# A delta-rule scan beside other matrix work: matmul-free steps tied to TensorE's chunk steps, gate rows in a buffer of their own, output weights split unscaled, MLP differences one step earlier

## The chip, the core and the metric

The kernel runs on one NeuronCore of a Trainium2 chip. The core has five engines that run side by side, each taking its own instructions in order: TensorE (PE in the profile; its weight loads are shown as PEld), VectorE (DVE), ScalarE (ACT), GpSimd (POOL) and SyncE (SP), which here issues all DMA transfers. The metric is the device time of one execution in microseconds (us); the time before is the median of three runs.

## What is computed

One layer of a hybrid block for 128 context tokens and 2048 latent tokens of width 1024. The mixer puts four heads of a gated delta-rule scan (run forwards and backwards) beside four groups of a spatially gated MLP, and both share an input and an output projection; a squared-ReLU MLP of width 4096 follows.

```python
def gated_delta_chunked(q, k, v, g, beta, s0):
    ...
    g = jnp.cumsum(to_chunks(g), axis=-1)
    diff = g[..., :, None] - g[..., None, :]
    decay = jnp.where(incl, jnp.exp(jnp.where(incl, diff, 0.0)), 0.0)
    a_mat = jnp.where(strict, jnp.einsum('bnhcd,bnhsd->bnhcs', k_beta, k) * decay, 0.0)
    sol = lax.linalg.triangular_solve(a_mat + jnp.eye(DN_CHUNK, dtype=f32), rhs, ...)
    ...
    def step(S, xs):
        v_new = u_c - jnp.einsum('bhck,bhkv->bhcv', w_c, S)
        o = jnp.einsum('bhck,bhkv->bhcv', qd, S) + jnp.einsum('bhcs,bhsv->bhcv', qk_c, v_new)
        S = S * jnp.exp(gl)[..., None, None] + jnp.einsum('bhck,bhcv->bhkv', kd, v_new)
...
    o_a = rmsnorm(o_a, o_norm_l) * jax.nn.silu(gate.reshape(B, T, H_A, DV))
    u = jax.nn.gelu(u)
    vg = layernorm_noaffine(jax.nn.gelu(vg)...)
    mixed = jnp.einsum('gts,bnsgc->bntgc', ws_l, vg) + bs_l.T[None, None, :, :, None]
    o_b = u * mixed
    out = jnp.concatenate([o_a, o_b], axis=-1)
    return out @ w_out_l, s_new
...
    x = x + ga1 * o
    h = rmsnorm(x, norm_ffn_l) * (1.0 + sc2) + sh2
    x = x + ga2 * (jnp.square(jax.nn.relu(h @ w_ff1_l)) @ w_ff2_l)
```

## The kernel before

**Number format.** A float32 operand is split into a high part `h` and a rest `lo`; a product takes three matmuls (high by high, high by rest, rest by high; `mm3`, L221 to L223). ACT casts the high part and DVE subtracts it to get the rest, for weights in `split_w` (L195, L196) as for activations.

**Three stages.** The first (to about 445 us) normalises the rows and projects q, k and v, with the convolution. The second (about 445 to 1270 us) is the scan with all that is woven into it, and it is where the change lies. The third is the MLP, whose products go by a seven-product scheme on halves; its operands are sums and differences of the normalised rows, made and stored in `hop_d` by `h2_steps`.

**The scan.** There are 34 units: 17 token tiles of 128 rows forwards, then the same backwards. Unit number i has *prep* steps, which solve the triangular system of its chunk without the state, and four *scan* steps, which need the state of unit i - 1. The first prep step makes `E`, the decays, out of a row of cumulated g that is broadcast to all partitions (ACT, L1016 and L1017) and masks it twice on POOL (`Es` L1019, `E` L1021). The second multiplies the key products `KK` by it (DVE, L1029), sets the diagonal (POOL, L1031), casts the result to float16 as `AH` (ACT, L1034) and cuts the first blocks out as `X` (DVE, L1035). The third turns `X` into `Y` on PE (L1041, evicted by ACT at L1043). Then come five levels of two steps each, every one a few small PE matmuls with an eviction that the next step needs: L1061 with the predicated copy `P` on DVE (L1065), and L1072 and L1075 with the casts of `Y` and `X` on ACT (L1076, L1077). Four more steps end in `T` (L1119, L1122). Below, the PE work of prep and scan steps is called a chunk step, and these matmuls chunk matmuls.

**What is woven in.** Forwards, PE's large share is fill: the projections for gate, v and u of the gMLP (`f2_steps`; 576 steps, 62 of them ahead of the scan), whose weights are `W2`. Backwards it is the output projection (`o_steps`, weights `WO`) and for tiles 9 to 16 the making of the MLP's operands (`h2_steps`; `put`, L877 to L880, casts, subtracts and stores a pair `opH`, `opL`, in the four staging buffers that raw weights use too).

**Order.** The order is written by hand as events with a time, in units of one scan unit (`at`, `spread`). Unit i's prep steps lie between i - 2.46 and i - 0.03 (backwards i - 2.63 and i + 0.06), evenly. A scheduler then places the instructions on the engines by event order, but lets any instruction go earlier that is ready earlier. `emit` ties what may not: the first PE instruction of a fill step stays behind the chunk matmul that was emitted last (or three back, in the backward half). Steps of other kinds that issue no PE instruction (the first prep step, weight splits, `put`s) have no such tie. A tie makes no wait on the chip; it sets the order in which instructions stand in the engines' queues.

**Loads.** Rows of g (for `E`) and of exp g (for turning q, L1153) both come through `load_rows`, three buffers of one tag. The eight u weights are loaded and split at -8.5, ahead of the scan. The sixteen output weights are loaded, multiplied by a column of scales on DVE (L194) and split between 17.58 and 18.3, where the forward half ends. Each load waits for a staging buffer (four of them) and, in order, for whatever stands ahead of it in SP's queue.

Of the kernel before, what the change touches and what calls it, by code (L numbers as in the profile page):

```python
# [18 lines left out]
P = 128  # L19
# [38 lines left out]
AHEAD = 3  # L58
WINDOWS = [2.46, 0.03, -0.51, 1.06, -1.61, 18.16, 17.58, 18.3,
# [4 lines left out]
def hybrid_step(  # L64
# [55 lines left out]
    nhalf = cp.tile([P, 80], F32, name="nhalf")  # L120
# [42 lines left out]
    wscale = cp.tile([P, KT], F32, name="wscale")  # L163
# [25 lines left out]
    def split_w(raw, scale=None, pool=None, tag="w"):  # L189
# [3 lines left out]
        if scale is not None:  # L193
            V.tensor_scalar_mul(raw, raw, scale)  # L194
# [4 lines left out]
    def load_split(src, scale=None):  # L199
        return split_w(raw_w(src, sp, "raw"), scale)  # L200

    W2 = {"g": [], "v": [], "u": []}

    def load_w2(gi, k):
        off = {"g": 1536, "v": 2576, "u": 2064}[gi]
        W2[gi].append(load_split(w_in[0, k * P : (k + 1) * P, off : off + 512]))
# [75 lines left out]
    with ExitStack() as ph:  # L282
# [432 lines left out]
        def second_mods():  # L715

            load(out=wsT, in_=w_spatialT)
            V.tensor_copy(wscale[:, 0:4], vec[:, 68:69].to_broadcast([P, 4]))
            V.memset(wscale[:, 4:8], 0.5)
# [102 lines left out]
    def h2_steps(t, psum, tmp, wide=w512, part=None, half=None, src=None, own=None):  # L822
# [107 lines left out]
    with ExitStack() as ph:  # L930
# [26 lines left out]
        def load_rows(src, t, d):  # L957
            gb = q32("gb", 3)
# [22 lines left out]
        def unit(t, d, fresh=False, last=False):  # L981
# [11 lines left out]
            def prep_loads():  # L993
                u["gb"] = load_rows(g_d, t, d)
# [5 lines left out]
            def scan_loads():  # L1000
# [6 lines left out]
                u["eg"] = load_rows(eg_d, t, d)  # L1007
# [18 lines left out]
            def _():  # L1026
                a = u["KK"]
                for h in range(H):
# [3 lines left out]
                                base=0, channel_multiplier=-1)  # L1032
                u["AH"], u["AL"], u["X"] = f16("AH", BA), f16("AL", BA), f16("X", BX)
                A.copy(u["AH"], a)  # L1034
# [271 lines left out]
        def o_steps(du):  # L1306
# [22 lines left out]
            def trans(half):  # L1329
                def f():  # L1330
# [11 lines left out]
                    A.copy(hs, ps)  # L1342
                    V.tensor_tensor(out=ls, in0=ps, in1=f32(hs), op=ALU.subtract)
# [97 lines left out]
        for gi in "vu":  # L1441
# [555 lines left out]
```

## Time and profile before

| | |
|---|---|
| median of three runs | 2627.44 us (2621.16 to 2628.88) |
| the profiled execution's own time | 2625.06 us |
| its span in the trace | 2623.1 us |
| mean granted clock of PE in it | 0.994 |
| PE's share of the chain that ended last | 81% |

The trace is of one execution. In the tables of stretches, each engine's busy time stands in us, then the number of instructions in brackets; PEclk is the clock that PE was granted, 1.00 being full speed; then the share of the DMA engines' time and GB/s. In lists of instructions the columns are start, duration, engine, line and operation, output<-input, shape, count, and in square brackets how long that engine stood idle before it and what released it. In groups of instructions the total busy time in us and the mean in ns follow the count. In lists of waits stand the total, how often, and the longest.

### The profile page before, as it was taken

The page shows a single profiled execution, that of the slowest core. Times are in us where ns is not written, and L with a number is a line of the kernel's source. Part 1 is how long each engine was busy: PE and PEld are TensorE (multiplying, and loading weights), DVE is VectorE, ACT ScalarE, POOL GpSimd, SP SyncE. Part 2 cuts the span into 40 slices and gives each one's busy share as a digit, 9 for nine tenths or more (in the row PEclk, how much of TensorE's full clock was granted, in tenths as well). Part 3 has the DMA queues.
Part 4 walks back from the last instruction along what each step waited for, and adds up shares of the span by engine and source line. Part 5 has one row for each costly group of instructions (what it writes and reads, how often), then busy time and mean ns, then how long its engine had stood idle before and what let it go on. Part 6 is the DMA issues. An engine that isn't in the chain of part 4 may idle for free.

```text
span 2623.1 us, 44123 instructions
## 1 busy us (share of the span) xinstructions
PE 2566.0 (98%) x15330; PEld 2150.2 (82%) x15330; DVE 1777.2 (68%) x3605; ACT 1238.7 (47%) x3086; POOL 253.4 (10%) x478
## 2 busy tenths in 40 slices
PE   8999999899999999899999999999999999999998
PEld 4899999688888778778888788888887888888887
DVE  5867745666667778786578786677675544774874
ACT  4655555555556557664245543333342432342441
POOL 3112112111112122111000000000000000000000
PEclk9999999999999999999999999999999999999999
DMA  8867637645556658896777879445369978786782
GB/s 298 285 213 220 198 110 234 217 152 163 167 167 180 191 186 246 256 281 186 279 235 236 249 229 328 146 137 152 118 204 370 338 265 281 263 255 213 237 262 94
DMA packets 533861, 579.79 MB, mean 221 GB/s; under 512 B 35500, under 2 KB 366684, under 8 KB 530054
## 3 DMA queue, kind: packets, MB, share of 16 engines
q1 hardware_dynamic: 533638, 576.98, 68.9%
q8 instruction: 120, 1.97, 0.3%
q14 instruction: 103, 0.84, 0.1%
HBM read 397.62 MB, written 179.22 MB: 220 GB/s over the span
## 4 chain that ended last, share of the span: by engine, by line
PE 81%; DMA 8%; DVE 4%; ACT 3%; issue 2%; SPq 1%; POOL 0%; DVEq 0%; POOLq 0%; ACTq 0%
PE f L221 15%; PE f L222 15%; PE f L223 15%; PE pj L221 7%; PE pj L223 6%; PE pj L222 6%; PE pd L991 3%; PE pm L221 1%; PE pm L223 1%; PE pm L222 1%; DMA r<-in_w_ff_dram 1%; PE pt L590 1%; PE pd L1176 1%; PE pd L1175 1%; DMA raw<-in_w_mod_dram 1%
## 5 line engine op out<-in xcount | busy, mean ns | idle before, releaser
L221 PE MATMUL f<-hop,zH 128*128 128x512 f32 x960 | 373.7, 390 | 2.4 <-ACT zH L1500 2.4
L223 PE MATMUL f<-hop,zL 128*128 128x512 f32 x960 | 373.6, 389 | 0.0
L222 PE MATMUL f<-hop,zH 128*128 128x512 f32 x960 | 373.2, 389 | 0.0
L221 PE MATMUL f<-hop,wH 128*128 128x512 f32 x896 | 351.7, 393 | 2.4 <-ACT x L1576 2.4
L222 PE MATMUL f<-hop,wH 128*128 128x512 f32 x896 | 349.5, 391 | 0.0
L223 PE MATMUL f<-hop,wL 128*128 128x512 f32 x896 | 344.7, 390 | 0.0
L1500 ACT CAST zH<-zraw 128x512 fp32r<-128x512 f32 x240 | 146.9, 620 | 290.8 <-DVE zraw L1494 89.4
L221 PEld LDWEIGHTS f<-hop,zH 128*128 128x128 f32 x960 | 180.2, 188 | 41.2 <-ACT zH L1500 4.0
L223 PEld LDWEIGHTS f<-hop,zL 128*128 128x128 f32 x960 | 180.2, 188 | 39.0 <-DVE zL L1494 1.7
L222 PEld LDWEIGHTS f<-hop,zH 128*128 128x128 f32 x960 | 180.2, 188 | 37.2
L1494 DVE TENSOR_TENSOR zL<-zraw,zH 128x512 fp32r<-128x512 f32 x240 | 162.7, 688 | 68.7 <-ACT zH L1500 55.9
L221 PEld LDWEIGHTS f<-hop,wH 128*128 128x128 f32 x896 | 168.8, 188 | 36.6 <-ACT x L1576 2.8
L223 PEld LDWEIGHTS f<-hop,wL 128*128 128x128 f32 x896 | 168.5, 188 | 35.6
L222 PEld LDWEIGHTS f<-hop,wH 128*128 128x128 f32 x896 | 169.0, 189 | 32.5
L223 PE MATMUL pj<-kH,wL 128*128 128x386 f32 (+2 forms) x568 | 190.5, 335 | 0.0
L221 PE MATMUL pj<-kH,wH 128*128 128x386 f32 (+2 forms) x568 | 189.1, 335 | 0.3 <-DVE kH L488 0.3
L222 PE MATMUL pj<-kL,wH 128*128 128x386 f32 (+2 forms) x568 | 189.3, 333 | 0.0
L180 POOL TENSOR_TENSOR r<-rsq,nhalf 128x1 f32<-128x1 f32 (+1 forms) x38 | 22.8, 600 | 1379.1 <-DVE rsq L179 1379.1
L1647 ACT CAST wH<-s 128x512 fp32r<-128x512 f32 x96 | 58.9, 620 | 173.0 <-DVE s L1494 173.0
L538 DVE SCALAR_TENSOR_TENSOR cv<-pj,vec,cv 128x384 f32<-128x384 f32 (+2 forms) x164 | 87.2, 539 | 58.2 <-ACT cv L535 56.8
L1065 DVE CAST_PREDICATED P<-om,pd 128x256 f16<-128x256 uint16 x170 | 71.0, 428 | 64.4 <-PE pd L1061 63.5
L221 PEld LDWEIGHTS pj<-kH,wH 128*128 128x128 f32 x568 | 107.1, 189 | 4.6 <-issue 4.2
(409 smaller groups left out, 5889.8 us busy)
## 6 DMA issues: line engine op xcount, KB each, us to landing
zraw<-z_d SPq DMA_DIRECT2D x212, 256.0 KB, 4.6
raw<-in_w_ff_dram SPq DMA_DIRECT2D x128, 256.0 KB, 4.8
hop<-hop_d SPq DMA_DIRECT2D x28, 1024.0 KB, 11.4
z_d<-c SPq DMA_DIRECT2D x96, 256.0 KB, 2.4
zraw<-s_d SPq DMA_DIRECT2D x96, 256.0 KB, 5.0
raw<-in_w_mod_dram SPq DMA_DIRECT2D x80, 256.0 KB, 4.3
r<-in_w_ff_dram SPq DMA_DIRECT2D x80, 256.0 KB, 5.3
s_d<-s SPq DMA_DIRECT2D x64, 256.0 KB, 3.2
```

Of the source, the lines that this page charges most:

```text
L221: T.matmul(ps, lh, rh, start=first and i == 0, stop=False, skip_group_check=more)
L222: T.matmul(ps, lh, rl, start=False, stop=False, skip_group_check=more)
L223: T.matmul(ps, ll, rh, start=False, stop=last and i == n - 1, skip_group_check=more)
L538: V.scalar_tensor_tensor(out=cv[:, o : o + m], in0=ps[:, s + sh : s + sh + m], scalar=convw[:, w, j : j + 1], in1=cv[:, o : o + m], op0=AL ...
L590: T.matmul(ps[:, i * P : (i + 1) * P], kTt[:, i * P : (i + 1) * P], rhs[:, i * P : (i + 1) * P], start=True, stop=True)
L991: T.matmul(p[:, h, :], lhs[:, h, :], rhs[:, h, :], start=True, stop=True)
L1065: V.copy_predicated(out=half(u["P"], yi), mask=half(bc4(om[s]).bitcast(U16), yi), data=pp)
L1175: T.matmul(p[:, h, :], u["qT"][:, h, :], s[:, h, :], start=True, stop=False)
L1176: T.matmul(p[:, h, :], u["QK"][:, h, :], u["vn"][:, h, :], start=s is None, stop=True)
L1494: V.tensor_tensor(out=out, in0=a, in1=b, op=op)
L1500: A.copy(h, src)
L1647: A.copy(h, s2)
```

## The change

1. **Ties for steps without matmuls.** In `emit`, a step that issues no PE instruction and isn't fill now gets, for each of its DVE, ACT and POOL instructions, the same kind of tie: behind the first PE instruction of the chunk step emitted last.
2. **The second prep step is cut in two**, so that the cast to `AH` and the making of `X` form a step of their own; a unit then has 18 prep steps, not 17, in the same stretch.
3. **Rows of g** get a tag of their own (`gr`, one buffer, in the pool that holds the prep tiles); rows of exp g keep three (`eg`).
4. **Weights.** `wscale` and its multiplications go. Three raw weights are loaded at -8.5; then one weight is split at a time, u from -2 on and the output weights from 16.4 on, 0.12 units apart, and each split issues the next load. The scale moves into the eviction of the transposed rows in `o_steps`: ACT's cast becomes an activation with a scale, DVE's subtraction a scalar_tensor_tensor.
5. **MLP differences.** In `h2_steps` each subtraction stands one step earlier than the `put` that needs it.

```diff
+COMPUTE = (mybir.EngineType.DVE, mybir.EngineType.Activation, mybir.EngineType.Pool)
...
-    def split_w(raw, scale=None, pool=None, tag="w"):
+    def split_w(raw, pool=None, tag="w"):
...
-        if scale is not None:
-            V.tensor_scalar_mul(raw, raw, scale)
         A.copy(h, raw)
         V.tensor_tensor(out=lo, in0=raw, in1=f32(h), op=ALU.subtract)
...
         def plain():
             put(1, u[0])
             put(2, u[1])
+            u["d"] = part("d")
+            sub(u["y"][1], u["y"][0], u["d"])
 
         def third():
             put(3, u["y"][1])
-            d = part("d")
-            sub(u["y"][1], u["y"][0], d)
-            put(7, d)
+            put(7, u["d"])
+            sub(u["y"][0], u[0])
 
         def fifth():
-            sub(u["y"][0], u[0])
             put(5, u["y"][0])
+            sub(u["y"][1], u["y"][0])
 
         def sixth():
-            sub(u["y"][1], u["y"][0])
             put(6, u["y"][1])
+            sub(u[1], u["y"][1])
 
         def fourth():
-            sub(u[1], u["y"][1])
             put(4, u[1])
...
             def prep_loads():
-                u["gb"] = load_rows(g_d, t, d)
+                u["gb"] = load_rows(g_d, t, d, "gr", 1, pp)
...
-                u["eg"] = load_rows(eg_d, t, d)
+                u["eg"] = load_rows(eg_d, t, d, "eg", 3)
...
+
+            @prep.append
+            def _():
                 u["AH"], u["AL"], u["X"] = f16("AH", BA), f16("AL", BA), f16("X", BX)
-                A.copy(u["AH"], a)
+                A.copy(u["AH"], u["KK"])
                 V.tensor_tensor(out=u["X"], in0=u["AH"], in1=bc4(sg2), op=ALU.mult)
...
-        def load_wo(n, k):
-            if k == 0:
+        wlist = [("u", k) for k in range(KT)] + [(n, k) for n in range(2) for k in range(KT)]
+        wraw = []
+
+        def ahead():
+            if len(wraw) < len(wlist):
+                n, k = wlist[len(wraw)]
+                src = w2_src(n, k) if n == "u" else w_out[0, k * P : (k + 1) * P, n * 512 : (n + 1) * 512]
+                wraw.append(raw_w(src, sp, "raw"))
+
+        def split_next(j):
+            n, k = wlist[j]
+            if n != "u" and k == 0:
                 ga1.append(wrow(mod_d[1:2, 2 * D + n * 512 : 2 * D + n * 512 + 512]))
                 WO.append([])
-            WO[n].append(load_split(w_out[0, k * P : (k + 1) * P, n * 512 : (n + 1) * 512], wscale[:, k : k + 1]))
+            (W2 if n == "u" else WO)[n].append(split_w(wraw[j]))
+            ahead()
...
-                    A.copy(hs, ps)
-                    V.tensor_tensor(out=ls, in0=ps, in1=f32(hs), op=ALU.subtract)
+                    scale = 0.5 if half else vec[:, 68:69]
+                    A.activation(hs, ps, AF.Copy, scale=scale)
+                    V.scalar_tensor_tensor(out=ls, in0=ps, scalar=scale, in1=f32(hs), op0=ALU.mult, op1=ALU.subtract)
...
-        for gi in "vu":
-            for k in range(NV if gi == "v" else 0, KT):
-                at(-9 if gi == "v" else -8.5, lambda gi=gi, k=k: load_w2(gi, k))
+        for k in range(NV, KT):
+            at(-9, lambda k=k: load_w2("v", k))
+        for _ in range(3):
+            at(-8.5, ahead)
+        for j in range(len(wlist)):
+            at(-2 + 0.12 * j if j < KT else 16.4 + 0.12 * (j - KT), lambda j=j: split_next(j))
...
-        spread(p2[6], p2[7], [lambda n=n, k=k: load_wo(n, k) for n in range(2) for k in range(KT)], None)
...
             f()
+            made = tc.nc.cur_bb.bb.instructions[start:]
+            pe = [x for x in made if x.engine == mybir.EngineType.PE]
+            if hist and not pe and kind != "fill":
+                for x in made:
+                    if x.engine in COMPUTE:
+                        tc.add_manual_dep(x, hist[-1].name, mybir.DependencyInfo(
+                            mybir.DependencyClass.NoSync, mybir.DependencyReason.DATA), reason="order")
```

More of the change, by code (lines that the diff above doesn't have):

```diff
@@ L119, in hybrid_step @@
     V.tensor_copy(ident16, ident)
-    nhalf = cp.tile([P, 80], F32, name="nhalf")
+    nhalf = cp.tile([P, 88], F32, name="nhalf")
     V.memset(nhalf, -0.5)
@@ L197, in split_w, with load_split, w2_src @@
         return h, lo
-    def load_split(src, scale=None):
-        return split_w(raw_w(src, sp, "raw"), scale)
+    def load_split(src):
+        return split_w(raw_w(src, sp, "raw"))
     W2 = {"g": [], "v": [], "u": []}
+    def w2_src(gi, k):
+        off = {"g": 1536, "v": 2576, "u": 2064}[gi]
+        return w_in[0, k * P : (k + 1) * P, off : off + 512]
     def load_w2(gi, k):
-        off = {"g": 1536, "v": 2576, "u": 2064}[gi]
-        W2[gi].append(load_split(w_in[0, k * P : (k + 1) * P, off : off + 512]))
+        W2[gi].append(load_split(w2_src(gi, k)))
     def w512(name, dt=F32):
```

8 lines of the change are left out of this document (2 added, 6 removed).

## The prediction

> **What bounds the kernel now.** I read the page's first part, then busy time by stretches of the scan stage, then PE's gaps one by one in the timeline, and last the list of waits.
>
> ```profile
> span 2623.1 us, 44123 instructions
> PE 2566.0 (98%) x15330; PEld 2150.2 (82%) x15330; DVE 1777.2 (68%) x3605; ACT 1238.7 (47%) x3086; POOL 253.4 (10%) x478
> ```
>
> PE is busy for 2566.0 of 2623.1 us, and the change takes no matmul away. What it can win is PE's idle time, and what PE loses by a slower clock around it. The stretches (row: length, then busy time of PE, PEld, DVE, ACT, POOL, then PE's clock):
>
> ```profile
> 470.00:490.00 20.00, 12.59 (x75) 9.12 (x74) 10.18 (x21) 8.36 (x20) 1.54 (x2) 0.74 0.80 269
> 510.00:600.00 90.00, 87.61 (x752) 72.07 (x751) 57.12 (x160) 51.89 (x144) 14.18 (x18) 1.00 0.52 158
> 600.00:860.00 260.00, 260.00 (x2268) 216.25 (x2267) 173.08 (x482) 146.87 (x397) 46.07 (x58) 1.00 0.57 169
> 860.00:950.00 90.00, 78.70 (x665) 63.00 (x664) 65.29 (x167) 49.23 (x135) 14.08 (x17) 0.94 0.65 210
> 1020.00:1200.00 180.00, 167.71 (x1460) 137.03 (x1458) 142.18 (x333) 125.18 (x385) 35.29 (x42) 0.99 0.87 272
> ```
>
> Idle time of PE, length less busy: 7.4 us at the start of the scan (call it A), 2.4 in 510 to 600 (B), 11.3 around the turn from forwards to backwards (C), 12.3 where tiles 16 to 9 run backwards (D); together 33.4. Clock loss, busy time by (1 - clock): A 12.59 x 0.26 = 3.3, C 78.70 x 0.06 = 4.7, D 167.71 x 0.01 = 1.7; together 9.7. So the ceiling of the gain is **43 us**. The 260 us between 600 and 860 have no idle time to give.
>
> **A.** The first unit's chain:
>
> ```profile
> 471.26 0.40 PE L1041 MATMUL pd<-ident,X 128*128 128x128 f16 x4
> 474.35 0.62 ACT L195 CAST wH<-raw 128x512 fp32r<-128x512 f32 x1 [2.76 <-DMA raw<-in_w_in_dram]
> 476.38 0.58 ACT L1043 CAST Y<-pd 128x512 f16<-128x512 f32 x1
> 477.01 0.37 PE L1061 MATMUL pd<-Y,AH 128*128 128x64 f16 x4 [5.35 <-ACT Y L1043]
> ```
>
> PE finished the `X` product at 471.66; its eviction (0.58 us) began only at 476.38, because a cast of a u weight stood ahead of it in ACT's queue, waiting for its transfer. Such waits, in the whole scan stage:
>
> ```profile
> ACT E L1016 <- DMA gb<-g_d: 58.5, 26, 5.9
> DVE d L883 <- DMA y<-h_d: 16.1, 4, 5.5
> DVE raw L194 <- DMA raw<-in_w_out_dram: 9.3, 8, 2.3
> ```
>
> All three are, like A's cast, instructions that went early and then held an engine that chunk steps need. But most of the 58.5 us fell where PE had fill enough: the stretch 600 to 860 shows it. So a wait that goes is worth only the gap of PE that it ends in.
>
> **The change part by part.** *Weights at A*: u is no longer split ahead of the scan, but one weight at a time with three loads in flight. Of the gap of 5.35 us the eviction itself must stay (0.58 us and a hand-over, say 0.8), and of the other 2 us of A I leave 0.5 for the next steps' own evictions. Best gain: 7.4 - 1.3 + 3.3 = 9.4. The fourth load is only issued at the first split, and the splits start just where PE has no fill; if ACT meets it as it met the old one, 2.76 us come back. I take **7** (range 3 to 9).
>
> *B*: ties keep a unit's `E` (four ACT instructions and an exp) from standing ahead of another unit's casts. I take **1.5** of 2.4.
>
> *Weights at C*:
>
> ```profile
> 865.48 0.48 DVE L194 TENSOR_SCALAR raw<-raw,wscale 128x512 f32<-128x512 f32 x1 [2.31 <-DMA raw<-in_w_out_dram]
> 866.97 0.28 PE L1072 MATMUL pd<-P,X 128*128 128x64 f16 x4 [0.86 <-DVE P L1065]
> 891.60 0.28 PE L1061 MATMUL pd<-Y,AH 128*128 128x64 f16 x4 [3.04 <-ACT Y L1076]
> 932.91 0.28 PE L1061 MATMUL pd<-Y,AH 128*128 128x64 f16 x4 [0.54 <-ACT Y L1043]
> 939.11 0.37 PE L1061 MATMUL pd<-Y,AH 128*128 128x64 f16 x4 [0.66 <-ACT Y L1076]
> ```
>
> DVE stood in the multiplication by the scale waiting for a weight, and the copy that PE needed came late. That wait goes with the multiplication, and the splits start at 16.4 instead of 17.58. The largest gap, 3.04 us, is mixed: DVE was busy with gMLP fill, which gets no tie, and one weight subtraction. The timeline's gaps of C that end behind an output weight or a waiting `E` (five, from the 0.86 to the 0.54 above) come to 2.7 us; those where such work is one of several (six, from the 3.04 to the 0.66) come to 7.3, of which I count half, as of the 4.7 of clock. 2.7 + 3.6 + 2.3 gives **8.5** of 16.0 (range 3 to 13).
>
> *The operations themselves*:
>
> ```profile
> L194 DVE TENSOR_SCALAR raw<-raw,wscale 128x512 f32<-128x512 f32 x16 | 8.1, 508 | 9.4 <-DMA raw<-in_w_out_dram 9.3
> L1343 DVE TENSOR_TENSOR oL<-pm,oH 128x512 fp32r<-128x512 f32 x21 | 14.3, 688 | 11.8 <-ACT oH L1342 11.7
> L1242 DVE SCALAR_TENSOR_TENSOR gw<-gw,pj 128x512 f32<-128x512 f32 x10 | 6.8, 682 | 6.3 <-ACT gw L1241 6.3
> ```
>
> Sixteen multiplications go, 8.1 us of DVE, in no other sum than C's. The eviction with a scale costs what it did: a scalar_tensor_tensor out of PSUM took 682 ns, the subtraction 688. ACT's scaled copy of this size is not in the trace; the cast and ACT's other 128x512 operations lie near 0.6 us, and I take 0 (between -1 and +3 us over 34 evictions, off the path while DVE follows ACT with slack).
>
> *The `put`s and differences at D*:
>
> ```profile
> 1024.42 0.28 PE L1061 MATMUL pd<-Y,AH 128*128 128x64 f16 x4 [0.34 <-ACT Y L1076]
> ...
> 1102.98 0.69 DVE L883 TENSOR_TENSOR d<-y 128x512 f32<-128x512 f32 x1 [5.50 <-DMA y<-h_d]
> 1106.13 0.50 PE L221 MATMUL pm<-wH,oH 128*128 128x512 f32 x1 [1.14 <-DVE tmp L1362]
> 1121.72 0.62 ACT L877 CAST opH<-d 128x512 fp32r<-128x512 f32 x1 [2.34 <-DMA hop_d<-opH]
> 1122.66 0.28 PE L1061 MATMUL pd<-Y,AH 128*128 128x64 f16 x4 [1.89 <-ACT Y L1076]
> ...
> 1172.99 0.28 PE L1072 MATMUL pd<-P,X 128*128 128x64 f16 x4 [1.42 <-DVE rr L1324]
> ```
>
> The difference waited 5.50 us for rows that had just been stored; the third pair waited for a staging buffer whose store was under way. Tied, the five steps keep their 0.42 units apart, about 9 us. The gaps of D behind a `put` (eight, from 1024.42 to 1172.99) come to 7.3 us, the one shown behind a difference is 1.1. Two pairs per step fill all four buffers, so a store that is slow may still be waited for: I take **8** of 14.0 (range 3 to 12). That the subtraction stands a step earlier moves 0.69 us on DVE and no more; the MLP stage, where the same function runs, is full on PE, and I count nothing there.
>
> *What the ties cost.* This is the open price. Before, a unit's `E` went far ahead of need:
>
> ```profile
> 695.76 1.28 ACT L1016 ACTIVATE E<-gb,gcol 128x128 f32<-128x128 f32 x4 [0.21 <-DMA gb<-g_d]
> 727.25 0.39 PE L1041 MATMUL pd<-ident,X 128*128 128x128 f16 x4
> ```
>
> That is one unit: 31 us from `E` to the `X` product. Tied, `E` starts three prep slots ahead of it. The work in between, in groups, and the matmul that ends the prep of each of the 34 units, with its first and last start:
>
> ```profile
> L1016 ACT ACTIVATE E<-gb,gcol 128x128 f32<-128x128 f32 x136 | 44.3, 393 | 71.2 <-DMA gb<-g_d 58.5 <-DMA vt_d<-tk 8.5 <-DVE P L1065 3.1
> L1017 ACT ACTIVATE E<-E 128x512 f32<-128x512 f32 x34 | 21.3, 628 | 0.3
> L1019 POOL TENSOR_SCALAR_AFFINE_SELECT Es<-E 128x512 f32<-128x512 f32 x34 | 22.1, 650 | 133.5 <-DVE QK L1079 60.7 <-ACT E L1017 51.8 <-DMA hL<-hL_d 12.4
> L1029 DVE SCALAR_TENSOR_TENSOR KK<-KK,nbeta,Es 128x128 f32<-128x128 f32 x136 | 47.6, 403 | 18.1 <-POOL Es L1019 16.6 <-DMA KK<-kk_d 1.5
> L1031 POOL TENSOR_SCALAR_AFFINE_SELECT KK<-KK 128x512 f32<-128x512 f32 x34 | 23.3, 685 | 46.6 <-DVE KK L1029 45.6 <-DMA gate_d<-gw 1.0
> L1034 ACT CAST AH<-KK 128x512 f16<-128x512 f32 x34 | 20.9, 616 | 34.9 <-POOL KK L1031 34.9
> L1035 DVE TENSOR_TENSOR X<-AH,sg 128x512 f16<-128x512 f16 x34 | 14.1, 416 | 2.5 <-ACT AH L1034 2.5
> ...
> L1119 PE MATMUL pd<-Y,ident x34: 379/379/631, 506.4 to 1247.2; 128*128 128x512 f16 x34
> ```
>
> A unit takes 740.8 / 33 = 22.4 us and a slot 22.4 x 2.43 / 18 = 3.0, so there are nine us. The work per unit, busy time over 34: 1.30 + 0.63 + 0.65 + 1.40 + 0.69 + 0.61 + 0.41 = 5.7 us, so 3.4 are left for queueing and hand-overs. If it isn't enough PE waits at the `X` product, and the fill behind it stands too. Bounds: 0, and 34 x 2 = 68 us if every unit came two late. The level steps live with slots just as short and leave no gap in the 260 us named, so I take near the lower end, 0.15 us a unit: **-5**.
>
> *Rows of g.* One buffer means that SP issues a unit's row only after ACT is through with the one before, 0.39 units (9 us) ahead of it by the events; behind that load stand the unit's `KK` and `QK` and then the scan loads. The user comes some 13 us after the issue, and the longest wait for such rows was 5.9. I count 0, as for the extra buffer.
>
> **Sum:** 7 + 1.5 + 8.5 + 8 - 5 = 20 us. The profiled execution took 2625.06 us, so 2605; the median of the runs is 2.4 higher, so **2607**.
>
> *A rule beside it.* PE's clock in a stretch with 2.56 us of idle time and behind the gap of 1.89 us shown above:
>
> ```profile
> 1070.00:1080.00 10.00, 7.44 (x64) 5.91 (x64) 7.88 (x21) 6.50 (x19) 1.02 (x1) 1.00 1.02 312
> 1124.00:1128.00 4.00, 4.00 (x28) 3.09 (x27) 3.00 (x9) 3.01 (x9) 0.00 (x0) 0.57 1.00 286
> ```
>
> The first left the clock at 1.00, the second was followed by 0.57. The Trainium skill, "TensorE: Matmul & The Clock Gate", section "Part 1: The HAM clock gate", says that the clock is halved after an idle window of about 3.4 us; by that only A's loss hangs on a gap, the 2.3 us of clock in C and about 1 in D wouldn't return, and the sum would be near 17. The trace disagrees: 1.89 us was enough here.
>
> **The rivals.**
> *The waits come back in another place.* A split still meets its transfer, a `put` its buffer; for it speaks that DMA is at 0.80 and 0.87 of its time in A and D. With the low ends, 3 + 1 + 3 + 3, less 5, the gain is about 5: 2622.
> *The ties move nothing.* They only order queues; where gMLP fill, untied, is what stood ahead, the gaps stay, and the rest pays for the ties: 2627, give or take 4. Against it: the rows of A and D name instructions that the ties do hold.
> *The prep chain comes too late.* PE waits at L1041 in every unit. With 1.1 us a unit, 34 x 1.1 = 37 against 25 won, it is slower by 12: 2639. It decides against the change from 25 / 34 = 0.74 us a unit, and is plainly slower from 1.0. For it: DVE is busy 142 of 180 us in D, and POOL works for other steps too. Against it: the level steps.
>
> **How the numbers follow.** My forecast (2594 to 2617) gets 0.52, the waits that come back 0.20, no movement 0.12, the late chain 0.16. A measurement of this kernel can tell 0.3%, some 8 us, from no change: faster is below 2619.5. The forecast is all faster, the second case half: 0.62. Same is the other half and nearly all of the third and a little of the last: 0.24. Slower 0.14. The range runs from 2592 to 2632: the forecast, the second and the third case, and not the late chain beyond its beginning.
>
> **What would show it.** Right: ACT's wait for g rows falls from 58.5 us to below 15; the eviction at L1043 of the first unit starts within 1 us of its matmul; no DVE or ACT wait above 2 us for raw weights; the two gaps at L1061 in D are gone; PE's idle time in the scan is below 18 us. Wrong: new waits of PE at L1041 for `X`, ACT waiting for a weight inside the scan, or PE's busy time itself grown, with chunk matmuls that wait on weight loads. A new gap where the splits at 16.4 meet the last gMLP products would sink C's term.

## The result, and the profile after

| | before | after |
|---|---|---|
| median of the runs compared | 2627.76 us (2621.16 to 2628.88, 4 runs) | 2613.3 us (2610.98 to 2615.75, 4 runs) |
| the profiled execution's own time | 2625.06 us | 2614.82 us |
| its span | 2623.1 us | 2613.0 us |

The ratio of after to before is 0.9951, with a 95% interval of 0.9937 to 0.9966: faster by some 14 us, where 20 were forecast. The experiments ran in several sessions, in which the median of the kernel before lay between 2621.7 and 2627.8, so kernels of different sessions are compared by their ratio to before, and stretches inside a kernel by its profile, which is of one execution. The times that the experiments expected make no allowance for the sessions, so a time that falls into its range says less than a stretch that does.

The page's first part, of after:

```profile
span 2613.0 us, 44092 instructions
PE 2569.1 (98%) x15330; PEld 2138.9 (82%) x15330; DVE 1767.7 (68%) x3587; ACT 1243.1 (48%) x3086; POOL 254.5 (10%) x478
```

The span is 10.1 us shorter, but PE's busy time is **3.1 us longer** than before's 2566.0, with the same 15330 instructions. The stretches of after, as they were shown of before (length, busy time of PE, PEld, DVE, ACT, POOL, PE's clock):

```profile
470.00:490.00 20.00, 14.87 (x95) 10.92 (x93) 12.66 (x34) 10.28 (x24) 1.90 (x3) 0.91 0.79 256
510.00:600.00 90.00, 88.68 (x741) 70.18 (x741) 54.95 (x154) 49.72 (x134) 13.66 (x18) 1.00 0.51 156
600.00:860.00 260.00, 256.44 (x2172) 202.04 (x2171) 165.94 (x462) 140.66 (x377) 44.96 (x58) 1.00 0.53 161
860.00:950.00 90.00, 85.44 (x749) 69.21 (x747) 71.25 (x181) 57.65 (x161) 17.60 (x20) 1.00 0.73 236
1020.00:1200.00 180.00, 173.00 (x1530) 142.58 (x1530) 148.07 (x350) 135.04 (x408) 40.22 (x45) 1.00 0.92 280
```

A, C and D gained: idle time fell from 7.4 to 5.1, from 11.3 to 4.6 and from 12.3 to 7.0 us, and the clock loss of the three together from 9.7 to 1.3 (A alone: 14.87 x 0.09). But look at 600 to 860, the stretch that had nothing to give: PE ran 2268 matmuls there before and 2172 now. The kernel is late there, and only 3.56 of the 260 us are idle.

To place the loss, the scan stage is cut at T(i), the start of the matmul that ends the prep of unit i (L1119 before, L1121 after; one per unit, 34 in all, read from the timeline). Units 0 to 16 run forwards. The last column but one runs from T(33) to the end. In us, from each kernel's own profile:

```
                  T0     T0-T4  T4-T16 T16-T20 T20-T25 T25-T33 T33-end   span
before          506.41   88.37  260.82   99.73  112.09  179.74 1375.94  2623.1
after           504.96   89.08  272.85   89.81  109.12  174.35 1372.83  2613.0
difference       -1.45   +0.71  +12.03   -9.92   -2.97   -5.39   -3.11   -10.1
```

All but the forward middle adds up to about 22 us won; the middle gives 12.0 back.

Individual gaps. The timeline of after at A (PE and ACT):

```profile
472.91 0.40 PE L1043 MATMUL pd<-ident,X 128*128 128x128 f16 x4
...
473.35 0.58 ACT L1045 CAST Y<-pd 128x512 f16<-128x512 f32 x1 [9.56 <-PE pd L1043]
473.98 0.28 PE L1063 MATMUL pd<-Y,AH 128*128 128x64 f16 x4 [0.67 <-ACT Y L1045]
...
476.05 0.60 ACT L1243 ACTIVATE gw<-pm 128x512 f32<-128x512 f32 x1 [2.12 <-DMA gate_d<-gw]
476.54 1.13 ACT L193 CAST wH<-raw 128x512 fp32r<-128x512 f32 x2
477.99 0.28 PE L1063 MATMUL pd<-Y,AH 128*128 128x64 f16 x4 [2.02 <-ACT Y L1078]
```

The eviction now follows its matmul at once (473.35 after 472.91 + 0.40); the gap of 5.35 us is one of 0.67. One level of the chain later stands a new one of 2.02: ACT stood first at an activation of the gMLP's fill (L1243), which has no tie and waited 2.12 us for a store, and then cast two u weights, which are now split right there.

This early eviction is not what the change gives every time. The new times of the weights and the ties are also in experiments 1, 2, 6 and 8 to 12 below, and in the trace of each of these that same activation stands ahead of the first eviction; PE's first gap is 3.1 to 4.4 us again. In experiment 6, which changes only the buffers of the rows:

```profile
473.01 0.60 ACT L1243 ACTIVATE gw<-pm 128x512 f32<-128x512 f32 x1 [13.08 <-DMA gate_d<-gw]
473.51 0.58 ACT L1045 CAST Y<-pd 128x512 f16<-128x512 f32 x1
474.14 0.37 PE L1063 MATMUL pd<-Y,AH 128*128 128x64 f16 x4 [4.41 <-ACT Y L1045]
```

From the first `X` product to T(0), the end of the first unit's prep (defined below), these eight take 32.9 to 36.4 us; before takes 35.15, after 32.05.

The list of waits of after over the scan stage (total, times, longest):

```profile
PE pd L1074 <- DVE P L1067: 7.8, 13, 1.4
DVE x L851 <- DMA x_d<-x: 7.7, 5, 2.7
...
ACT E L1015 <- DMA gr<-g_d: 5.1, 1, 5.1
```

ACT's waits for rows of g fell from 58.5 us to 5.1, the waits of the differences for `h_d` and those for raw output weights are no longer in it. The wait at L851, DVE scaling `x` in place and held by the store of that same `x`, came to only 0.4 us before. PE's gaps of after in C and D, by its timeline, the three longest:

```profile
919.66 0.28 PE L1074 MATMUL pd<-P,X 128*128 128x64 f16 x4 [1.14 <-DVE P L1067]
...
1114.39 0.28 PE L1074 MATMUL pd<-P,X 128*128 128x64 f16 x4 [1.42 <-DVE r L1334]
...
1173.10 0.22 PE L1111 MATMUL pd<-Y,AH 128*128 128x128 f16 x1 [1.51 <-DVE Y L1104]
```

Neither gap at L1061 that was shown of D has a successor.

### Where the 12 us went

The same stretch, T(4) to T(16), in the same view, first of before, then of after:

```profile
594.78:855.60 260.82, 260.82 (x2279) 217.43 (x2277) 174.01 (x487) 147.11 (x396) 46.07 (x58) 1.00 0.57 168
```

```profile
594.04:866.89 272.85, 269.30 (x2283) 213.05 (x2280) 174.37 (x484) 147.44 (x396) 45.49 (x58) 1.00 0.53 160
```

Same work (2279 and 2283 matmul records), same clock, 3.56 us more idle time and **8.5 us more busy time**. PE's timeline shows how the same matmuls can take longer. Before, from 700.20 on:

```profile
700.60 0.22 PE L1110 MATMUL pd<-Y,AL 128*128 128x128 f16 x1
700.62 0.48 PE L221 MATMUL pj<-wH,hH 128*128 128x512 f32 x1
700.94 0.39 PE L222 MATMUL pj<-wL,hH 128*128 128x512 f32 x1
701.17 0.39 PE L223 MATMUL pj<-wH,hL 128*128 128x512 f32 x1
701.40 0.39 PE L221 MATMUL pj<-wH,hH 128*128 128x512 f32 x1
```

and after, with two of the weight loads (PEld):

```profile
700.22 0.40 PE L224 MATMUL pj<-wH,hL 128*128 128x512 f32 x1
700.46 0.29 PE L1074 MATMUL pd<-P,X 128*128 128x64 f16 x4
700.59 0.28 PE L1077 MATMUL pd<-X,P 128*128 128x64 f16 x4
700.68 0.19 PEld L222 LDWEIGHTS pj<-wH,hH 128*128 128x128 f32 x1
700.71 0.48 PE L222 MATMUL pj<-wH,hH 128*128 128x512 f32 x1
701.02 0.40 PE L223 MATMUL pj<-wL,hH 128*128 128x512 f32 x1
701.02 0.19 PEld L224 LDWEIGHTS pj<-wH,hL 128*128 128x128 f32 x1
701.26 0.39 PE L224 MATMUL pj<-wH,hL 128*128 128x512 f32 x1
```

From one fill matmul to the next start lie 0.23 us inside a run of fill (701.17 to 701.40), but 0.31 to 0.32 from the first that follows a chunk matmul (700.62 to 700.94, 700.71 to 701.02). Before, PE went from chunk to fill 114 times in this stretch; after, 175 times, one triple of fill at a time. 61 x 0.09 = 5.5 us by this alone; the distances of all fill matmuls together, idle time taken out, grew by 7.9 us (158.7 to 166.6), most of the rest at the last matmul of each run of fill (on average 0.248 us in place of 0.234), and those of chunk matmuls by 0.5. With the longer distance goes a late weight load: that of a run's first fill matmul starts only 0.03 us ahead of it (700.68 for 700.71), that of a later one 0.23 (701.02 for 701.26; both are the medians of the stretch), and a load takes 0.19 us. That this makes the whole of the 0.09 is not shown.

**Theory S**, formed from this: the extra prep step did it. 17 steps lay in 2.43 units, 1/7 of a unit apart, so steps of neighbouring units fell on the same place and their chunk matmuls went back to back. 18 steps lie 0.135 apart, neighbours' steps fall between each other, and each gets fill on both sides. **Rivals:** the tied chain makes PE late (the -5 of the prediction, mis-sized), or the new order of the weights does it.

### The profile page after: what moved, and what is told of

It is laid out like the page before. It is cut to its first block, busy times and chain, and to the rows that moved or that the text cites. A ratio compares the mean times of both kernels' runs of the same rounds, so it can differ in the third digit from the quotient of the medians.

```text
span 2613.0 us, 44092 instructions
## 1 busy us (share of the span) xinstructions
PE 2569.1 (98%) x15330; PEld 2138.9 (82%) x15330; DVE 1767.7 (68%) x3587; ACT 1243.1 (48%) x3086; POOL 254.5 (10%) x478
## 4 chain that ended last, share of the span: by engine, by line
PE 86%; DMA 6%; DVE 4%; ACT 2%; issue 1%; SPq 1%; POOL 0%; DVEq 0%; POOLq 0%; ACTq 0%
PE f L222 15%; PE f L223 15%; PE f L224 15%; PE pj L222 7%; PE pj L224 7%; PE pj L223 7%; PE pd L990 3%; PE pm L222 2%; PE pm L224 2%; PE pm L223 2%; DMA r<-in_w_ff_dram 1%; PE pd L1178 1%; PE pt L591 1%; PE pd L1177 1%; DMA raw<-in_w_mod_dram 1%
```

## The experiments

All twelve in one table, as above; the last column is the ratio to before with its interval.

```
                  T0    T0-T4  T4-T16 T16-T20 T20-T25 T25-T33 T33-end   ratio  95%
before           506.4   88.4   260.8    99.7   112.1   179.7  1375.9
after            505.0   89.1   272.9    89.8   109.1   174.4  1372.8  0.9951 0.9937-0.9966
1 merge          506.1   86.0   261.7    92.8   111.0   177.8  1371.5  0.9937 0.9925-0.9950
2 stretch 2.571  504.8   86.7   264.1    91.4   108.6   175.2  1372.2  0.9922 0.9909-0.9936
3 before + cut   505.7   90.8   276.4   100.9   119.1   183.2  1374.7  1.0105 1.0091-1.0119
4 no ties        504.3   89.1   271.5    91.4   113.9   179.8  1371.5  0.9982 0.9972-0.9992
5 old weights    505.8   90.0   272.9    97.6   110.8   174.1  1371.5  0.9998 0.9989-1.0006
6 shared rows    505.7   88.3   272.8    90.0   109.3   174.0  1369.4  0.9969 0.9958-0.9980
7 late diffs     502.6   89.4   272.9    89.8   107.6   183.2  1375.0  1.0013 1.0005-1.0022
8 scan aligned   506.0   86.1   262.5    90.0   108.6   173.0  1371.7  0.9924 0.9912-0.9937
9 stretch 2.69   506.7   87.5   268.2    89.9   109.1   172.7  1373.9  0.9950 0.9936-0.9963
10 x apart       506.8   85.8   262.6    91.6   107.6   172.5  1383.8  0.9944 0.9931-0.9956
11 wider back    505.8   86.0   262.5    95.2   108.3   171.1  1383.6  0.9962 0.9950-0.9975
12 ties on fill  506.5   85.9   262.5    91.1   120.5   190.7  1378.2  1.0045 1.0032-1.0058
```

**1. The second prep step whole again** (17 steps, all else as after).

```diff
-            @prep.append
-            def _():
                 u["AH"], u["AL"], u["X"] = f16("AH", BA), f16("AL", BA), f16("X", BX)
```

> The changed kernel with the second prep step whole again: 17 prep steps per unit, not 18; ties, weights, rows of g and MLP differences as changed. Theory S (switches): with 17 steps in 2.43 units the steps are 1/7 of a unit apart, so chunk steps of neighbouring units fall on the same time and go back to back; with 18 they fall between each other, and PE changes from chunk matmuls to fill 175 times instead of 114 in the forward units 5 to 16, about 0.13 us each, plus 3.6 us of idle time. Undone, that stretch gets 8 to 12 us shorter: 2601 to 2606 us, with 114 switches and a unit of 21.6 us there. Rival K (the ties make E and X late, which is what costs the 12 us): X has one slot less than in the changed kernel, so PE waits more: 2613 to 2620, a unit there of 22.5 us or more.

The median was 2608.76 us. T(4) to T(16) is back at 261.7 with 114 switches, as S says; so it was neither the ties nor the weights. The time came out higher than S expected because of the backward half. PE's waits in 910 to 1240:

```profile
PE pd L1040 <- DVE X L1034: 14.6, 10, 2.8
```

L1040 is the `X` product, L1034 the making of `X`. This is the prediction's rival of a prep chain that comes too late, at 1.46 us each time (14.6 / 10). With the cut this wait does not exist backwards (after has one at this place in the whole stage, 1.8 us at 489.20): the third slot that the cut gives pays there and costs in the forward half.

**2. The cut kept, the forward stretch widened** so that 18 steps are 1/7 of a unit apart again (2.571 / 18 = 0.143).

```diff
-WINDOWS = [2.46, 0.03, ...
+WINDOWS = [2.601, 0.03, ...
```

> The changed kernel with its 18 prep steps spread over 2.571 units forwards (the first window 2.601 in place of 2.46), so that the steps are 1/7 of a unit apart again; nothing else is changed. Theory S: the switches fall back to about 118 in the forward units 5 to 16 and the stretch loses 8 to 12 us: 2601 to 2606. Rival K: E and X have a slot of 3.2 us in place of 3.0, so a little of the lateness goes: 2610 to 2613.

Measured 2604.62 us (2603.56 to 2606.96), in S's range. By the view of stretches, T(4) to T(16):

```profile
591.42:855.56 264.14, 261.87 (x2282) 214.94 (x2280) 179.33 (x486) 148.40 (x397) 47.62 (x58) 1.00 0.56 167
```

One number changed; 118 switches instead of 175, and 261.87 us busy instead of 269.30.

**3. Before with the cut alone.**

```diff
+
+            @prep.append
+            def _():
                 u["AH"], u["AL"], u["X"] = f16("AH", BA), f16("AL", BA), f16("X", BX)
-                A.copy(u["AH"], a)
+                A.copy(u["AH"], u["KK"])
```

> The kernel before with nothing but the second prep step cut in two (18 steps); no ties, weights as before. Theory S: the switches rise from 114 to 175 in the forward units 5 to 16, 6 to 10 us more: 2634 to 2638. Rival K: without ties E and X are early, so the cut costs nothing: 2625 to 2630.

Measured 2652.41 us, slower than both theories: the ratio is 1.0105. The middle has 175 switches and 269.7 us busy, as after, but 6.7 us idle where after has 3.6, and T(20) to T(33) lost 10.5 us. Without ties or the new weights the cut costs more, not less.

**4. After without ties.**

```diff
-            if hist and not pe and kind != "fill":
+            if False:
```

> The changed kernel without the ties for steps that issue no PE instruction; the cut, the weights, the rows of g and the MLP differences stay. Theory S: the units of the forward middle stay near 22.3 us (175 switches), and what the ties won, about 10 us where tiles 16 to 9 run backwards and part of the gain at the turn, is lost: 2622 to 2628. Rival K: the forward middle goes back to 21.6 us a unit (12 us won), against the same loss: 2610 to 2617.

Measured 2619.36 us. The middle stayed (271.5), as S said; the ties cost there 1.3 us at most (272.85 - 271.52). T(16) to T(20) lost only 1.6, but T(20) to T(33) lost 10.2. In its list of waits in that stretch, DVE's waits that ties had removed are back:

```profile
DVE d L882 <- DMA y<-h_d: 10.0, 4, 3.6
DVE opL L877 <- DMA hop_d<-opL: 6.8, 6, 2.8
```

So D was won by the ties (with part 5 of the change, see 7), and the turn was not.

**5. After with the weights' old places** (u split at -8.5, output weights between 17.58 and 18.3; still without a scale). Each load is issued at its own split again, so the loads in flight ahead of the splits go as well.

```diff
         def split_next(j):
+            ahead()
...
             (W2 if n == "u" else WO)[n].append(split_w(wraw[j]))
-            ahead()
...
-        for k in range(NV, KT):
-            at(-9, lambda k=k: load_w2("v", k))
-        for _ in range(3):
-            at(-8.5, ahead)
-        for j in range(len(wlist)):
-            at(-2 + 0.12 * j if j < KT else 16.4 + 0.12 * (j - KT), lambda j=j: split_next(j))
+        for gi in "vu":
+            for k in range(NV if gi == "v" else 0, KT):
+                at(-9 if gi == "v" else -8.5, lambda gi=gi, k=k: load_w2(gi, k))
+        wlist[:] = wlist[KT:]
+        spread(p2[6], p2[7], [lambda j=j: split_next(j) for j in range(len(wlist))], None)
```

> The changed kernel with the weights loaded and split when the kernel before did it (u at -8.5, output weights each loaded and split between 17.58 and 18.3); the scale stays in the eviction, all else is as changed. Theory W (the weights' times won the turn): the chain from the end of unit 16's prep to that of unit 20 takes 97 to 101 us again in place of 89.8, and the kernel 2618 to 2624. Rival (the ties alone won the turn, the times are worth nothing): 90 to 93 us there, 2611 to 2616. For the start of the scan either theory says little: the first unit's T came only 1.5 us earlier with the new times.

Measured 2620.29 us. T(16) to T(20) lost 7.8 of the 9.9 us that after had won there. ACT's wait for output weights in that stretch, and two of PE's gaps:

```profile
ACT wH L193 <- DMA raw<-in_w_out_dram: 6.8, 5, 2.9
```

```profile
921.91 0.28 PE L1063 MATMUL pd<-Y,AH 128*128 128x64 f16 x4 [2.21 <-ACT Y L1078]
932.32 0.27 PE L1111 MATMUL pd<-Y,AH 128*128 128x128 f16 x1 [2.45 <-DVE Y L1104]
```

So the turn was won by when the weights are loaded and split; the places and the loads in flight, which go together here, are not told apart. It was not won by the multiplication that is gone, since this run lacks it too. At the start of the scan nothing can be told: T(0) is 505.84 here, and 502.6 to 506.8 in the kernels with the new times.

**6. Rows of g and of exp g in one tag again.**

```diff
-                u["gb"] = load_rows(g_d, t, d, "gr", 1, pp)
+                u["gb"] = load_rows(g_d, t, d, "gb", 3)
...
-                u["eg"] = load_rows(eg_d, t, d, "eg", 3)
+                u["eg"] = load_rows(eg_d, t, d, "gb", 3)
```

> The changed kernel with rows of g and of exp g sharing three buffers of one tag again. My reading is that the buffer is worth nothing once E is held back: 2611 to 2616. Rival: the shared buffers make the held E wait for its rows, at the place where all units need it: ACT's wait for g rows goes to over 20 us and the kernel to 2618 to 2630.

Measured 2612.98 us. No stretch of the scan in the table differs from after's by more than 0.8 us and the intervals overlap: nothing that these runs can tell. The rival's wait of ACT for rows of g didn't come: there is none in the scan stage.

**7. The MLP differences at their old steps.**

```diff
             put(2, u[1])
-            u["d"] = part("d")
-            sub(u["y"][1], u["y"][0], u["d"])
...
             put(3, u["y"][1])
-            put(7, u["d"])
-            sub(u["y"][0], u[0])
+            d = part("d")
+            sub(u["y"][1], u["y"][0], d)
+            put(7, d)
...
         def fourth():
+            sub(u[1], u["y"][1])
             put(4, u[1])
```

> The changed kernel with each MLP difference back in the step of the put that needs it; ties and all else as changed. My reading is that the ties, not the early differences, ended the waits for rows and buffers: 2610 to 2616, T of unit 20 to T of unit 33 in 282 to 286 us. Rival: the difference and its put in one tied step queue up on DVE and ACT: 2616 to 2622, that stretch 287 to 291 us.

I missed this one: 2625.42 us, all that the change had won. T(25) to T(33) lost 8.8 us (T(20) to T(33) 7.3, since T(20) to T(25) was 1.6 shorter), in these four gaps above all:

```profile
1068.67 0.28 PE L1074 MATMUL pd<-P,X 128*128 128x64 f16 x4 [3.12 <-DVE P L1067]
1093.53 0.28 PE L1074 MATMUL pd<-P,X 128*128 128x64 f16 x4 [1.60 <-DVE P L1067]
1117.80 0.37 PE L1074 MATMUL pd<-P,X 128*128 128x64 f16 x4 [2.42 <-DVE P L1067]
1143.07 0.28 PE L1074 MATMUL pd<-P,X 128*128 128x64 f16 x4 [2.03 <-DVE P L1067]
```

Some 5 us ahead of the first of them DVE stood at the scaling of `x` (untied, since it is fill) for its store, and then worked off what had piled up, the `P` last:

```profile
1063.71 0.49 DVE L851 TENSOR_SCALAR x<-x,r 128x512 f32<-128x512 f32 x1 [3.07 <-DMA x_d<-x]
```

Each of the four follows such a wait: in that stretch they come to 10.8 us in four here, and to 3.1 in two in after. So the subtraction's own 0.69 us is not the point; what waits in DVE's queue is. Why the store is awaited longer when the differences stand late is not shown. The traced execution (2622.2 us) is also one of the fastest of its eleven: by the ratios this kernel lost 0.6% against after, some 16 us, and the two traces hold 7.5 of them. With the late differences (before, 3 and 7) the part behind T(33) takes 1374.7 to 1375.9 us, in after and in 1, 2, 4, 5, 6, 8 and 9 1369.4 to 1373.9 (means 1375.2 and 1371.8): the MLP stage seems to have won some 3 us by them as well.

**8. Experiment 2, and the scan steps aligned** to the same grid.

```diff
-WINDOWS = [2.601, 0.03, -0.51, 1.06, ...
+WINDOWS = [2.601, 0.03, -0.60, 1.11, ...
```

> The second experiment's kernel (18 prep steps over 2.571 units forwards) with the four scan steps of a forward unit 0.4275 apart (from -0.60 to 1.11 in place of -0.51 to 1.06), near the grid of the prep steps. By its order PE changes from chunk matmuls to fill 91 times in the forward units 5 to 16, not 118. Theory S, 0.13 us a change: that stretch 3 to 4 us shorter than the 264.1 of the second experiment, 2600 to 2602. Rival (the price isn't in the changes but in how early chunk steps are ready): steps standing closer wait for each other, the stretch gets longer, 2605 to 2612.

Measured 2599.79 us (2598.22 to 2604.17), the lowest median of all. But T(4) to T(16) is only 1.6 us shorter than in 2, all of it idle time (2.27 to 0.27); the busy time there did not fall, though there are only 91 switches:

```profile
592.03:854.57 262.54, 262.27 (x2282) 220.04 (x2280) 178.29 (x486) 147.07 (x397) 46.17 (x58) 1.00 0.55 167
```

The fill did follow the switches: its distances shrank by 3.3 us for 27 fewer, 0.12 each, beside 0.13 from before to after (7.9 for 61). But the distances of chunk matmuls grew by 3.7, nearly all of it in float32 products of the scan steps, which are the steps that this edit moved (L990 and L1178: 41.1 to 45.0 us). Why these got slower is open. As ratios, 8 and 2 can't be told apart.

**9. Forward stretch 2.69 units**: still off the grid, with longer slots than experiment 2.

```diff
-WINDOWS = [2.46, 0.03, ...
+WINDOWS = [2.72, 0.03, ...
```

> The kernel after with one number changed: the forward steps (18, as after) are spread over 2.69 units instead of 2.43, so their distance is 0.158 of a unit, which is no fraction 1/n, as 2.43 over 17 is 1/7. Theory 'switches' (the 12 us lost in the middle of the scan come of the number of times PE goes from a chunk matmul to a fill matmul; in PE's order there are 170 of these in units 5 to 16 here, about as many as after's 175): T4 to T16 stays at 270 to 273 us and the time at 2611 to 2616 us. Theory 'grid' (the loss comes of steps of neighbouring units falling on the same place, which any distance off the grid removes): T4 to T16 is 262 to 266 us and the time 2602 to 2607 us.

(The distance is 2.69 / 18 = 0.149 of a unit; the 0.158 in the expectation was divided by 17. A unit's steps still fall between its neighbour's, 1 / 0.149 = 6.7.) Measured 2609.7 us, and 268.2 for the stretch: between the two theories' numbers, within neither.

```profile
594.16:862.36 268.20, 268.06 (x2279) 212.23 (x2277) 179.68 (x484) 146.79 (x395) 47.78 (x58) 1.00 0.55 163
```

It shows that the 12 us are two pieces. The idle time is gone (268.20 - 268.06) where the slots are longer, while the busy time is still high at 170 switches. (The slot's length alone doesn't set the idle time: 2 and 8 have the same slots, with 2.27 and 0.27 us.) Lined up by switches, the busy time of the stretch is 260.8 (114, before), 261.2 (114, exp. 1), 261.9 (118, 2), 268.1 (170, 9), 269.3 (175, after), 269.7 (175, 3) and 269.8 (175, 4): about 8 us for 60, 0.14 each. Only 8 (262.3 at 91) leaves the line. In all of these kernels the switches are few on the grid and many off it, so this line alone wouldn't tell their number from the grid; the distances of the fill matmuls do. The theory 'grid' as it was put, namely that falling on the same place costs, was at odds with experiment 2 already. By the ratio, 9 can't be told from after.

**10. Experiment 8, the scaled `x` in tiles of its own**, to be rid of the wait at L851.

```diff
+            raw = u["x"]
+            u["x"] = [wide("xs"), wide("xs")]
             for n in range(2):
-                V.tensor_scalar_mul(u["x"][n], u["x"][n], u["r"])
+                V.tensor_scalar_mul(u["x"][n], raw[n], u["r"])
```

> Experiment 8's kernel, and the scaled x of the gate goes to a tile of its own instead of over x, so that the scaling on DVE no longer waits for the store of x. Theory 'store' (DVE, held at this scaling for 2 to 3 us five times in the backward half after, comes late with r and P, and PE waits for them): DVE's waits for that store go from 7.7 us to 0, the gaps of PE for r and P get shorter, the time is 2595 to 2599 us beside experiment 8's 2600. Rival (PE's work hides these waits by now): 2598 to 2602 us, T20 to T33 within 1.5 us of experiment 8's 281.6.

Neither: 2607.4 us. The wait went from DVE's list (6.7 us in experiment 8), and T(20) to T(33) took 280.1 us beside 281.6: the rival's reading, it was hidden. But in this trace the MLP stage behind, which uses the same function, lost 12 us. Its waits of PE between 1270 and 1530, where 7.4 of them lie as idle time:

```profile
PE f L860 <- DVE xs L853: 4.3, 3, 3.2
PE f L222 <- ACT x L1600: 1.5, 1, 1.5
PE f L222 <- ACT wH L1671: 1.3, 1, 1.3
```

Experiment 8 has no idle time to speak of there (0.08). The two extra tiles per norm come out of the pool that the MLP's weights and products use too; that this shortage is the cause is likely, not shown. The traced execution is the slowest of its five (2612.87 us); by the ratios 10 lost 0.2% against 8, some 5 us, and the intervals overlap.

**11. Experiment 10 with a wider backward stretch.**

```diff
-           2.63, -0.06, ...
+           2.94, -0.06, ...
-            at(i - 3 if i > PL else -12.5, u["prep_loads"])
+            at((i - 3 if i <= NT else i - 3.4) if i > PL else -12.5, u["prep_loads"])
```

> Experiment 10's kernel with the backward steps spread over 2.94 units instead of 2.63, and the loads of a unit's rows put 0.4 of a unit earlier. In PE's order the switches from a chunk matmul to a fill matmul in the backward half go from 101 to 88. Theory 'switches': T16 to T33 1 to 2 us shorter than in experiment 10. Rival (more units under way at once, so that steps wait for tiles that are not free): 0 to 4 us longer, with new gaps of PE behind E or the rows.

The rival: T(16) to T(33) 374.5 us beside 371.7 in experiment 10, though there were fewer switches. All the loss lies at the turn (95.2 beside 91.6), where the first backward units now start earlier; in the whole scan stage PE waited 5.1 us for `X` in four waits, beside 1.9 in one.

**12. Experiment 8, fill without matmuls tied too.**

```diff
-            if hist and not pe and kind != "fill":
+            if hist and not pe:
```

> Experiment 8's kernel, with fill steps without matmuls tied behind PE's chunk step as well (after ties the scan's steps only). If untied fill steps that run ahead on DVE and ACT are what still makes chunk steps late: T20 to T33 shrinks by 2 to 5 us, the time is 2595 to 2598 us. Rival (late evictions of the fill keep PSUM tiles from PE): the time is 2602 to 2612 us, with PE gaps at fill matmuls that wait for ACT or DVE.

Worse than either: 2635.81 us. From T(20) to T(33) it took 311.2 us, 29.6 more than in experiment 8. The list of waits there:

```profile
DVE tmp L1376 <- PE pj L224: 24.0, 10, 6.0
...
PE pd L1074 <- DVE P L1067: 14.4, 13, 2.5
```

A tied eviction no longer goes when its product is ready; it holds its place in DVE's queue, DVE waits there up to 6.0 us for the fill matmul, and a `P` that PE needs stands behind it. So tying all of the fill wins nothing. Whether a single step would pay for a tie is not tried: the activation at L1243 still holds the first eviction here, with a gap of 3.8 us.

## Why the prediction came out as it did

The time, 2613.3, lies in the range, and 6 us above the point. By the terms of its sum (20 us expected, 10.1 in the profiled executions):

- **A, 7: mis-sized.** From the first `X` product to T(0) 35.15 us became 32.05, 3.1 won, the low end of the range; that product itself came 1.65 later (472.91), so T(0) is 1.45 earlier. The casts that held the eviction went as forecast. What I left for the next steps' own evictions, 0.5 us, was too little: ACT waited at a gMLP activation for its store and then cast u weights, a new gap of 2.02. And that even 3.1 were won is partly luck: in the traces of eight experiments with the same weights and ties this wait comes ahead of the first eviction, and the same way takes 32.9 to 36.4 us. I had priced only the weights' cast; the gMLP activation in the same queue waits for a transfer of its own.
- **B, 1.5: nothing.** Idle time in 510 to 600 fell by 1.1, but T(0) to T(4) took 0.7 longer. With the switches of after undone (experiment 1) it is 2.4 shorter than before.
- **C, 8.5: 9.9**, and by one of the two causes named: with the old places of the weights 7.8 of it are lost again (experiment 5), without ties 1.6 (experiment 4). The other, the multiplication that goes, did not show: experiment 5 lacks it too, and there ACT waits for the weights instead of DVE.
- **D, 8: 8.4** from T(20) to T(33), by the cause named, the ties (10.2 lost without them), but not by it alone.
- **The early subtraction, "0.69 us on DVE and no more": the wrong step.** Without it 7.3 us of T(20) to T(33) are lost, and 10.2 without ties, more together than the 8.4 that the change won there, so the two need each other. I priced the instruction, not what then waits in the queue. Some 3 us in the MLP stage, which I had at nothing, seem to be due to it too.
- **The ties' cost, -5: the wrong step.** 12.0 were lost, but the ties' part is at most 1.3 (experiment 4). The rest came of cutting the second prep step, which I had weighed only as giving the chain a third slot and had not priced in PE's order: 18 steps in 2.43 units raised PE's changes from chunk to fill from 114 to 175 (8.5 us of busy time) and made the slots short: of the 3.56 us of idle time 1.70 stay without ties (experiment 4), and 0.14 with longer slots (experiment 9). My argument from "no gap in the 260 us" could not see it, since PE's busy time itself grew. That sign stood in my list of what would make me wrong, but I had put it down to chunk matmuls; it was the fill's distances that grew.
- **Rows of g, 0: held**, as far as experiment 6 can tell. **The eviction with a scale, 0:** not tried alone; no wait in the lists points to it.

Of the signs: ACT's wait for g rows, the first eviction, the raw weights (longest wait inside the scan 0.9 us) and the two gaps at L1061 came as written. PE's idle time in the scan stage did not: 22.0 us from 380 to 1250 (33.6 before), not below 18. And the first eviction came so only in after and in experiment 7 among the kernels with ties and new weights, and the wait for g rows fell to 9.0 us without ties too (experiment 4).

Of the rivals, the late prep chain is real, but only where the cut is missing and the ties are there (experiment 1, backwards). In the profiled executions the sum fell short by 9.9: 5.5 at A, 2.2 at B and 7.0 in the middle, against 1.4 more at C, 0.4 at D and 3.1 in the tail.

Experiments 2 and 8, after with one and three numbers of the order's table changed, are the fastest: 0.9922 (0.9909 to 0.9936) and 0.9924 (0.9912 to 0.9937) of before, beside after's 0.9951 (0.9937 to 0.9966), whose interval begins where theirs end.

## What to carry to other kernels

When a step is added to chains that are interleaved by hand, ask where the steps of neighbouring chains now fall: count how often the busiest engine changes from one kind of work to the other, because a full engine shows no gap and still gets slower. An instruction that is moved can cost or win what stands behind it in its queue, many times its own duration. Here it paid to tie what ran ahead and then waited for a transfer, and not to tie evictions, which are free to go as soon as their product is there.

## What the runs showed of the hardware

The first fill matmul (128x512) behind a chunk matmul of at most 128 columns takes 0.31 to 0.34 us to the next start, a later one within a run 0.23. In the fill's distances together a change costs 0.12 to 0.13 us, from 91 changes in some 260 us to 175; by the busy time of the stretch 0.14 between 114 and 175, while from 118 to 91 nothing was left of it, since other matmuls got slower.

PE's granted clock fell without a long gap. In experiment 5, by stretches:

```profile
910.00:920.00 10.00, 8.30 (x80) 6.79 (x79) 8.64 (x27) 5.60 (x14) 1.48 (x2) 1.00 0.84 257
920.00:930.00 10.00, 7.57 (x66) 6.31 (x66) 8.70 (x24) 9.79 (x27) 3.15 (x5) 0.66 0.93 326
930.00:940.00 10.00, 7.68 (x39) 7.10 (x39) 8.73 (x17) 3.37 (x11) 0.49 (x1) 0.66 0.80 253
```

The gaps of over 0.5 us in there are those of 0.54, 0.85, 2.21 and 2.45 us; by shorter stretches the clock is 1.00 up to 922, 0.81 to 924 and 0.50 to 934, so it fell behind the third, with 3.25 us of idle time between 917 and 922. The Trainium skill, "TensorE: Matmul & The Clock Gate", section "Part 1: The HAM clock gate", puts the halving behind an idle window of about 3.4 us; here, as before at D, no single gap ahead of the fall was over 2.3 us. Nor does such a gap always do it: behind one of 2.29 us (before, 1073.44) the clock stayed at 1.00. What counts instead, these runs don't tell.
